# An arena of ten 16 KB pairs in place of twenty 8 KB blocks, with expert weights loaded four rows at a time

## The chip, the cores and the metric

One core of a Trainium2 chip. The time is device microseconds of one execution, the median of the runs; in the profile, times are microseconds from the start of the span unless marked ns.

## The reference, cut to what matters

One encoder layer for 256 tokens of width 1024, all in float32: two attention branches side by side, merged by gates, then 32 experts of which every token takes four.

```
mod = silu(c) @ w_ada + b_ada                      # 6 vectors: shift, scale, gate, twice
z = (x * (1 + scale1) + shift1) @ w_in             # q, k, v of A; compressed q, kv of B; two gates
y_a, y_b = chunked_attention(z), latent_attention(z)
merged = sigmoid(g_a) * (y_a @ w_branch_a) + sigmoid(g_b) * (y_b @ w_branch_b)
x = layer_norm(ALPHA * x + gate1 * (merged @ w_out))
h = x * (1 + scale2) + shift2
experts = top 4 of (h @ w_router + b_router), softmax weights
f = sum over the 4: weight * (swiglu(h @ w_gate[e], h @ w_up[e]) @ w_down[e])
out = layer_norm(ALPHA * x + gate2 * f)
```

The expert weights are 32 x 3 matrices of 1024 x 1024 float32, 4 MB each.

## The kernel before, in words

**The arena.** Nearly everything large that comes from memory, and many intermediates, live in one pool of `NB = 20` blocks of 8 KB per partition (1 MB each over 128 partitions). `al` takes the block that has been free longest (`freed` holds the count at which each was freed), `fr` gives blocks back, `hold(n)` sets n free blocks aside for a while. A load into a block waits for the last reader of what was in it before. Which block a load gets is settled when the program is written out; the order in which each engine's queue takes its instructions is set then too, by the framework's planner (`schedule_with_timeline_sim=True`), from its own estimate of times. All large loads are issued by SP, whose queue takes its instructions in order.

**Split matmuls.** In the mixers a float32 product is made of three matmuls of rounded halves (`mm3`, lines 278 to 281): `split` (lines 151 to 153) casts a block into a high part on ACT and subtracts it on DVE or POOL for the low part, so each weight block takes two more blocks.

**Mixers.** `load_start`, `modulate` and `project` make the first projections. Twelve `z_pair` steps follow, beside eight `attend` steps; each `ada2` step (line 627) loads two blocks of `w_ada`, which DVE adds into two accumulators `acc0` and `acc1` (line 640). The matmuls called `mod` (lines 706 and 707) reduce them, bank after bank, first the four of `acc0`, then those of `acc1`. Then `load_branch` (line 761) loads a quarter of both branch weights and splits it, four times, two ahead of the matmuls `ba` and `bb`; each quarter is merged with the gates `gT` (lines 796 to 799) into `mg`. `load_wo` (line 805) does the same with quarters of `w_out`; eight calls of `o_part` (line 836, two token halves, two column halves, two quarters) make `o`. Normalisation and routing follow, in a row of small steps.

**Experts.** All experts run as dense products over gathered tokens: group `s` of two experts, then `e0` to `e12` of two or three (`GROUPS`), each with the matrices `g`, `u` and `d` in turn. `load_group` (line 1006) issues the loads of one matrix of a group: for each of four quarters and each expert j one block of two rows per partition. A partition p holds the rows 8p to 8p+7 of a matrix, so two rows are 8 KB in one piece. `mm` (line 1056) goes through k = 0 to 7; each k takes 16 matmuls over the two column halves and the experts' token segments, and after every odd k it frees the blocks of that quarter:

```
                if k % 2 == 1:
                    for rg in regs:
                        fr(rg[k // 2])
```

After the `g` matrix of group `s`, `take_late` takes two blocks for good. The last load of the last group (`fine`) is cut in column halves. The loop over extra items (line 1322, `get_w`) runs only where an expert has more tokens than its slots.

Of the kernel before, what the change touches and what calls it, by code (L numbers as in the profile page):

```python
# [8 lines left out]
F32 = mybir.dt.float32  # L9
# [8 lines left out]
P = 128  # L18
# [14 lines left out]
NB = 20  # L33
# [37 lines left out]
def tile_layer(  # L71
# [49 lines left out]
    freed = {i: i - NB for i in range(NB)}  # L121
    clock = [0]

    def al(dt=F32):
        assert freed, "no block is free"
        i = min(freed, key=freed.get)
        del freed[i]
        clock[0] += 1
        return ar.tile([P, BLK], dt, tag=f"blk{i}", bufs=1, name=f"blk{i}_{clock[0]}"), i
# [9 lines left out]
    def fr(*blocks):  # L139
        for i in blocks:  # L140
            clock[0] += 1
            assert i not in freed
            freed[i] = clock[0]
# [60 lines left out]
    hTh_v, hTh_r = al(F32R)  # L204
    hTl_v, hTl_r = al(F32R)
# [109 lines left out]
    def project(b):  # L315
        wv = LS[b][1]
        ws = []
        for kk in range(2):
            hi, hr = al(F32R)
            lo, lr = al(F32R)  # L320
            split(wv[kk][0][:, 0:NZ], hi[:, 0:NZ], lo[:, 0:NZ], "VG"[kk])
            fr(wv[kk][1])
            ws.append((hi, lo, hr, lr))
        for kk in range(2):
            k = 2 * b + kk
            hi, lo, hr, lr = ws[kk]
# [4 lines left out]
            fr(hr, lr)  # L331
# [41 lines left out]
    def split_cols(L, n, pieces=2, engs="VG"):  # L373
        w, r = L
        hv, hr = al(F32R)
        lv, lr = al(F32R)
        hi = hv.rearrange("p (k m) -> p k m", k=8)
        lo = lv.rearrange("p (k m) -> p k m", k=8)
        st = 8 // pieces
        for i in range(pieces):  # L380
            sl = slice(i * st, (i + 1) * st)
            split(w[:, sl, :], hi[:, sl, :], lo[:, sl, :], engs[i % len(engs)])
        fr(r)
        return hi, lo, (hr, lr)
# [176 lines left out]
    yT, yT_r, gT, gT_r = [None, None], [], [], []  # L561

    def take_yT(br):
        v, r = al(F32R)
        yT[br] = v.rearrange("p (s j n) -> p s j n", s=2, j=4)
        yT_r.append(r)
# [77 lines left out]
    def z_pair(name, dst):  # L644
        W = split_cols(loads[name], 256, 4, "GVGG" if name[0] == "g" else "GVGV")
        ps = ps_g(name)
        for j in range(2):
            z_T(W, j, ps[:, j * S:(j + 1) * S])
        A.copy(dst, ps.rearrange("p (j n) -> p j n", j=2))
        fr(*W[2])  # L650
# [19 lines left out]
    fr(hTh_r, hTl_r, qk_r, bva[0][1], bva[1][1])  # L670
# [85 lines left out]
    hold(4)  # L756
# [4 lines left out]
    def load_branch(jp):  # L761
        v, r = al()
        v = v.rearrange("p (b k m) -> p b k m", b=2, k=4)
        for br, w in enumerate((w_branch_a, w_branch_b)):
            SP.dma_start(v[:, br, :, :], w[0].rearrange("(k p) m -> p k m", p=P)[:, :, jp * 256:(jp + 1) * 256])
        hv, hr = al(F32R)
        lv, lr = al(F32R)
# [5 lines left out]
        WB.append((hi, lo, hr, lr))  # L773
# [3 lines left out]
    mgh_v, mgh_r = al(F32R)  # L777
    mgl_v, mgl_r = al(F32R)
    mgh = mgh_v.rearrange("p (j n) -> p j n", j=8)
    mgl = mgl_v.rearrange("p (j n) -> p j n", j=8)  # L780
    for jp in range(4):
# [8 lines left out]
        fr(WB[jp][2], WB[jp][3])  # L790
# [9 lines left out]
    fr(*yT_r, *gT_r)  # L800
# [4 lines left out]
    def load_wo(hf, i):  # L805
# [3 lines left out]
        hv, hr = al(F32R)  # L809
        lv, lr = al(F32R)  # L810
# [6 lines left out]
        WO.append((hi, lo, hr, lr))  # L817
# [130 lines left out]
    for i in range(2):  # L948
        for t in range(2):
            o_part(t, 0, i)  # L950
        fr(*WO[i][2:4])
        load_wo(1, i)
# [7 lines left out]
    for i in range(2):  # L960
        o_part(1, 1, i)
        fr(*WO[2 + i][2:4])
# [18 lines left out]
    fr(mgh_r, mgl_r, rt_r, ms_r, rwa_r, rwb_r)  # L981
# [12 lines left out]
    def take_late():  # L994
        if not late:
            a, b = al()[0], al()[0]
# [30 lines left out]
    def expert_group(nm, segs, slots, wcol, get_w, get_bias, hooks=(), end=None):  # L1027
# [28 lines left out]
        def mm(stat, kind, name):  # L1056
# [4 lines left out]
            def step(k, hf):  # L1061
                for c0, m, par in segs:
                    T.matmul(pss[hf][c0:c0 + m, :], stat[:, k, c0:c0 + m],  # L1063
                             ch[par][k // 2][:, k % 2, hf * 512:(hf + 1) * 512],
                             start=(k == 0), stop=(fine and k == 7), skip_group_check=True)

            for k in range(8):
# [8 lines left out]
                if k % 2 == 1:  # L1076
                    for rg in regs:
                        fr(rg[k // 2])
# [230 lines left out]
    with tc.For_i(0, n_items) as it:  # L1309
# [60 lines left out]
```

## Time and profile before

| | |
|---|---|
| Runs | 1250.84, 1247.3, 1252.55 us; median 1250.84 |
| The profiled execution | 1245.99 us, span 1244.3 us |
| Mean granted TensorE clock | 0.966 of full speed |
| PE, DVE, ACT, POOL busy | 1103.0, 362.8, 172.5, 123.0 us |
| Bytes read from memory | 459.09 MB |
| Expert loads | 128 + 128 + 126 loads of 1,024 KB, 4 of 512 KB |

In a timeline a line gives start, duration, engine and line of the code, operation, the tile written and the tiles read, shape, and in square brackets the idle time before it with what ended it. All blocks of the arena appear as `blk`. A line of a group has busy time and mean duration in ns of one behind the first bar, and behind the second the idle time just before. `SPq` is the load queue. DMA share is the mean busy share of 16 DMA engines; it can exceed 1. The queue line of the packets gives packets, MB and that share.

### The profile page before, as it was taken

What the parts mean: (1) busy time and instruction counts of PE and PEld (TensorE: products, weight loads), DVE (VectorE), ACT (ScalarE), POOL (GpSimd) and SP (SyncE); (2) the same over time, 40 slices, a digit from 0 to 9 for tenths busy, and PEclk for the clock granted to TensorE, in tenths of its full rate; (3) what the DMA queues carried; (4) which work ended last, traced back from release to release, by engine and by line L of the source; (5) the groups of instructions that cost most, each with busy time, mean ns of one, the idle gap of its engine ahead of it and who ended that gap; (6) DMA issues with size and microseconds to landing.
All of it is one profiled execution on the core that took longest, in us unless ns stands there. A gap on an engine that the chain in (4) does not pass through costs nothing.

```text
span 1244.3 us, 19465 instructions
## 1 busy us (share of the span) xinstructions
PE 1103.0 (89%) x8023; PEld 511.9 (41%) x8023; DVE 362.8 (29%) x704; ACT 172.5 (14%) x340; POOL 123.0 (10%) x140
## 2 busy tenths in 40 slices
PE   6889999797998989899989789889889999899995
PEld 4658885773242433434223223232233434343431
DVE  4868982684121121211012001011011211111113
ACT  3345552230000000000000000000000000000011
POOL 2211562433000000000000000000000000000001
PEclk8989998898999999899999999999999999999998
DMA  9958646398999999999999999999999999999992
GB/s 341 345 186 307 229 142 237 102 355 333 421 420 420 421 422 420 422 420 420 421 421 421 421 420 421 422 421 420 422 421 421 421 420 421 420 420 421 421 399 76
DMA packets 90333, 461.44 MB, mean 371 GB/s; under 512 B 8809, under 2 KB 33430, under 8 KB 39298
## 3 DMA queue, kind: packets, MB, share of 16 engines
q1 hardware_dynamic: 90242, 460.17, 91.6%
q8 instruction: 64, 1.05, 0.3%
q14 instruction: 27, 0.22, 0.0%
HBM read 459.09 MB, written 1.05 MB: 370 GB/s over the span
## 4 chain that ended last, share of the span: by engine, by line
DMA 48%; PE 36%; DVE 8%; issue 3%; SPq 2%; ACT 1%; POOL 1%; DVEq 0%; ACTq 0%; POOLq 0%
DMA blk<-in_w_down_dram 19%; DMA blk<-in_w_up_dram 14%; DMA blk<-in_w_gate_dram 13%; DVE blk L640 1%; PE e2d L1063 1%; PE e0d L1063 1%; PE sg L1063 1%; PE e12d L1063 1%; PE e3d L1063 1%; PE e1d L1063 1%; PE sd L1063 1%; PE e3u L1063 1%; PE e2u L1063 1%; PE e1u L1063 1%; PE e0u L1063 1%
## 5 line engine op out<-in xcount | busy, mean ns | idle before, releaser
L153 POOL TENSOR_TENSOR blk<-blk,blk 128x512 fp32r<-128x512 f32 (+2 forms) x44 | 84.8, 1948 | 148.8 <-ACT blk L152 80.5
L1298 POOL COPY sel<-sel 96x64 bf16<-96x64 bf16 (+2 forms) x30 | 5.9, 230 | 807.5 <-PE e5d L1132 90.4
L152 ACT CAST blk<-blk 128x512 fp32r<-128x512 f32 (+2 forms) x76 | 54.1, 767 | 41.5 <-DVE blk L798 16.6
L1092 ACT ACTIVATE blk<-blk 128x512 f32<-128x512 f32 x28 | 17.2, 630 | 234.0 <-DVE blk L1090 234.0
L153 DVE TENSOR_TENSOR blk<-blk,blk 128x512 fp32r<-128x512 f32 (+2 forms) x32 | 39.0, 1227 | 33.7 <-ACT blk L152 23.0
L640 DVE SCALAR_TENSOR_TENSOR blk<-blk,csil,blk 128x1024 f32<-128x1024 f32 x28 | 41.8, 1537 | 1.3 <-DMA blk<-in_w_ada_dram 1.2
L281 PE MATMUL g<-blk,blk 128*128 128x256 f32 x128 | 36.6, 291 | 2.0 <-POOL blk L153 2.0
L279 PE MATMUL g<-blk,blk 128*128 128x256 f32 x128 | 36.8, 288 | 0.0
L280 PE MATMUL g<-blk,blk 128*128 128x256 f32 x128 | 36.1, 282 | 0.0
L1063 PE MATMUL e7u<-blk,xgb 128*32 128x512 f32 x128 | 25.3, 599 | 4.5 <-DMA blk<-in_w_up_dram 4.5
L1063 PE MATMUL e5u<-blk,xgb 128*32 128x512 f32 x128 | 25.6, 599 | 4.0 <-DMA blk<-in_w_up_dram 4.0
L1063 PE MATMUL e6u<-blk,blk 128*32 128x512 f32 x128 | 25.3, 599 | 4.0 <-DMA blk<-in_w_up_dram 4.0
L1063 PE MATMUL e5d<-blk,xgb 128*32 128x512 f32 x128 | 23.2, 656 | 3.6 <-DMA blk<-in_w_down_dram 3.4
L281 PEld LDWEIGHTS g<-blk,blk 128*128 128x128 f32 x128 | 24.2, 191 | 4.3 <-POOL blk L153 2.9
L1063 PE MATMUL e7d<-blk,blk 128*32 128x512 f32 x128 | 22.7, 597 | 3.0 <-DMA blk<-in_w_down_dram 2.7
L279 PEld LDWEIGHTS g<-blk,blk 128*128 128x128 f32 x128 | 24.5, 191 | 0.9 <-issue 0.6
L1063 PE MATMUL e6d<-blk,xgb 128*32 128x512 f32 x128 | 22.4, 621 | 2.5 <-DMA blk<-in_w_down_dram 2.5
L1063 PE MATMUL e4d<-blk,blk 128*32 128x512 f32 x128 | 22.1, 613 | 2.8 <-DMA blk<-in_w_down_dram 2.8
L280 PEld LDWEIGHTS g<-blk,blk 128*128 128x128 f32 x128 | 24.5, 191 | 0.0
L1063 PE MATMUL e4u<-blk,xgb 128*32 128x512 f32 x128 | 20.6, 596 | 2.0 <-DMA blk<-in_w_up_dram 2.0
L1063 PE MATMUL e6g<-blk,blk 128*32 128x512 f32 x128 | 19.4, 596 | 1.8 <-DMA blk<-in_w_gate_dram 1.8
L1063 PE MATMUL e7g<-blk,xgb 128*32 128x512 f32 x128 | 19.4, 595 | 1.7 <-DMA blk<-in_w_gate_dram 1.7
(745 smaller groups left out, 1919.2 us busy)
## 6 DMA issues: line engine op xcount, KB each, us to landing
blk<-in_w_gate_dram SPq DMA_DIRECT2D x128, 1024.0 KB, 19.7
blk<-in_w_up_dram SPq DMA_DIRECT2D x128, 1024.0 KB, 19.8
blk<-in_w_down_dram SPq DMA_DIRECT2D x126, 1024.0 KB, 19.8
blk<-in_w_ada_dram SPq DMA_DIRECT2D x24, 1024.0 KB, 9.6
blk<-in_w_in_dram SPq DMA_DIRECT2D x12, 1024.0 KB, 5.4
blk<-in_w_in_dram SPq DMA_DIRECT2D x8, 592.0 KB, 11.4
blk<-in_w_out_dram SPq DMA_DIRECT2D x4, 1024.0 KB, 6.0
blk<-in_w_branch_a_dram SPq DMA_DIRECT2D x4, 512.0 KB, 3.7
```

The source lines that it names most:

```text
L152: A.copy(hi, src)
L153: (V if eng == "V" else G).tensor_sub(lo, src, hi.bitcast(F32))
L279: T.matmul(o, sh, mh, start=first, stop=False)
L280: T.matmul(o, sh, ml, start=False, stop=False)
L281: T.matmul(o, sl, mh, start=False, stop=last)
L640: eng.scalar_tensor_tensor(acc_v[:, sl], v[:, q * D:(q + 1) * D], csil[:, k:k + 1], acc_v[:, sl], op0=ALU.mult, op1=ALU.add)
L1063: T.matmul(pss[hf][c0:c0 + m, :], stat[:, k, c0:c0 + m], ch[par][k // 2][:, k % 2, hf * 512:(hf + 1) * 512], start=(k == 0), stop=(fine an ...
L1092: A.activation(s, g[:, sl], AF.Sigmoid, scale=SW_ALPHA)
L1298: G.tensor_copy(sel[:, lo:lo + n], sel96[:, r:r + 1].to_broadcast([96, n]))
```

## The change

The arena becomes ten pairs of 16 KB per partition. `al2` takes a whole pair, the one free longest. `al` takes a half of a broken pair if there is one, the one freed first among these, else it breaks the next pair. `fr` joins two free halves to a pair again; `fr2` frees a pair. High and low part of a split come from one pair (`hi_lo`); both `yT` and the two late blocks are pairs too; `hold` counts pairs. Expert weights are loaded four rows per partition at a time, 16 KB in one piece and 2 MB a load, and freed after k = 3 and k = 7. In the last group's `fine` matrix the second half is loaded as two rows and then two column halves of two rows.

```diff
-    freed = {i: i - NB for i in range(NB)}
+
+    freed = {i: i - NB for i in range(0, NB, 2)}
+    half = {}
+    pair = {}
     clock = [0]

-    def al(dt=F32):
-        assert freed, "no block is free"
+    def al2(dt=F32):
+        assert freed, "no pair of blocks is free"
         i = min(freed, key=freed.get)
         del freed[i]
         clock[0] += 1
-        return ar.tile([P, BLK], dt, tag=f"blk{i}", bufs=1, name=f"blk{i}_{clock[0]}"), i
+        pair[i] = ar.tile([P, 2 * BLK], dt, tag=f"blk{i}", bufs=1, name=f"blk{i}_{clock[0]}")
+        return pair[i], i
+
+    def al():
+        if half:
+            i = min(half, key=half.get)
+            del half[i]
+        else:
+            i = al2()[1]
+            half[i + 1] = clock[0]
+        return pair[i & ~1][:, (i & 1) * BLK:(i & 1) * BLK + BLK], i
+
+    def fr2(*pairs):
+        for i in pairs:
+            clock[0] += 1
+            assert i not in freed and i % 2 == 0 and i not in half and i + 1 not in half
+            freed[i] = clock[0]
+
+    def fr(*blocks):
+        for i in blocks:
+            clock[0] += 1
+            assert i not in half and (i & ~1) not in freed
+            if i ^ 1 in half:
+                del half[i ^ 1]
+                freed[i & ~1] = clock[0]
+            else:
+                half[i] = clock[0]

...
-    def fr(*blocks):
-        for i in blocks:
-            clock[0] += 1
-            assert i not in freed
-            freed[i] = clock[0]
+    def hi_lo():
+        v, i = al2(F32R)
+        return v[:, 0:BLK], v[:, BLK:2 * BLK], i
...
-            hi, hr = al(F32R)
-            lo, lr = al(F32R)
+            hi, lo, hr = hi_lo()
...
-    yT, yT_r, gT, gT_r = [None, None], [], [], []
+    yT, gT, gT_r = [None, None], [], []
+    yT_v, yT_r = al2(F32R)
...
-    hold(4)
+    hold(2)
...
-        hv, hr = al(F32R)
-        lv, lr = al(F32R)
+        hv, lv, hr = hi_lo()
...
-        fr(WB[jp][2], WB[jp][3])
+        fr2(WB[jp][2])
...
-            a, b = al()[0], al()[0]
+            ab = al2()[0]
+            a, b = ab[:, 0:BLK], ab[:, BLK:2 * BLK]
...
-        for kq in range(4):
+        for kh in range(2):
             for j in range(n):
-                v, r = al()
-                v = v.rearrange("p (k n) -> p k n", k=2)
-                if not (fine and kq == 3):
-                    SP.dma_start(v, aps[j][:, 2 * kq:2 * kq + 2, :])
+                v, r = al2()
+                v = v.rearrange("p (k n) -> p k n", k=4)
+                if not (fine and kh == 1):
+                    SP.dma_start(v, aps[j][:, 4 * kh:4 * kh + 4, :])
+                else:
+                    SP.dma_start(v[:, 0:2, :], aps[j][:, 4:6, :])
                 ch[j].append(v)
                 regs[j].append(r)
         if fine:
             for hf in range(2):
                 sl = slice(hf * 512, (hf + 1) * 512)
                 for j in range(n):
-                    SP.dma_start(ch[j][3][:, :, sl], aps[j][:, 6:8, sl])
+                    SP.dma_start(ch[j][1][:, 2:4, sl], aps[j][:, 6:8, sl])
...
-                             ch[par][k // 2][:, k % 2, hf * 512:(hf + 1) * 512],
+                             ch[par][k // 4][:, k % 4, hf * 512:(hf + 1) * 512],
                              start=(k == 0), stop=(fine and k == 7), skip_group_check=True)

             for k in range(8):
@@ -1073,9 +1100,9 @@
                 elif not (fine and k == 7):
                     for hf in range(2):
                         step(k, hf)
-                if k % 2 == 1:
+                if k % 4 == 3:
                     for rg in regs:
-                        fr(rg[k // 2])
+                        fr2(rg[k // 4])
...
-            for kq in range(4):
-                v, r = al()
-                v = v.rearrange("p (k n) -> p k n", k=2)
-                SP.dma_start(v, src[:, 2 * kq:2 * kq + 2, :])
+            for kh in range(2):
+                v, r = al2()
+                v = v.rearrange("p (k n) -> p k n", k=4)
+                SP.dma_start(v, src[:, 4 * kh:4 * kh + 4, :])
```

## Rows read from the trace of the kernel before

**Rows 1.** The page: DMA rate in 40 slices; the chain that ended last.

```profile
GB/s 341 345 186 307 229 142 237 102 355 333 421 420 420 421 422 420 422 420 420 421 421 421 421 420 421 422 421 420 422 421 421 421 420 421 420 420 421 421 399 76
...
DMA 48%; PE 36%; DVE 8%; issue 3%; SPq 2%; ACT 1%; POOL 1%; DVEq 0%; ACTq 0%; POOLq 0%
```

**Rows 2.** By stage: PE, PEld, DVE, ACT, POOL busy; clock, DMA share, GB/s.

```profile
60.00:190.00 130.00, 121.81 (x870) 101.89 (x869) 109.84 (x212) 68.21 (x177) 51.72 (x34) 0.97 0.63 221
190.00:293.00 103.00, 83.27 (x440) 63.86 (x439) 62.33 (x124) 32.25 (x45) 45.34 (x28) 0.87 0.66 246
293.00:589.00 296.00, 276.81 (x2386) 108.28 (x2390) 56.56 (x122) 17.40 (x30) 2.77 (x14) 0.98 1.00 413
```

**Rows 3.** Waits of the load queue, 285 to 320 us.

```profile
SPq L1014 <- PE sg L1063: 7.3, 2, 7.0
```

**Rows 4.** DMA packets, 14 to 18 us, then 400 to 1200 us.

```profile
DMA packets 1387, 1.41 MB, mean 351 GB/s; under 512 B 18, under 2 KB 1386, under 8 KB 1387
...
q1 hardware_dynamic: 1387, 1.41, 110.2%
...
DMA packets 46166, 336.59 MB, mean 421 GB/s; under 512 B 5123, under 2 KB 5123, under 8 KB 5123
...
q1 hardware_dynamic: 46111, 335.79, 101.0%
```

**Rows 5.** Timeline of the load queue SP, 176 to 300 us.

```profile
189.20 0.40 SPq L765 DMA_DIRECT2D blk<-in_w_branch_a_dram  x1
...
220.15 0.37 SPq L765 DMA_DIRECT2D blk<-in_w_branch_a_dram  x1
...
236.56 14.31 SPq L808 DMA_DIRECT2D blk<-in_w_out_dram  x4
...
298.71 0.80 SPq L1014 DMA_DIRECT2D blk<-in_w_down_dram  x2
```

**Rows 6.** Timeline of PE: `sg` (293 to 312 us), last `e12u` matmuls.

```profile
293.40 8.72 PE L1063 MATMUL sg<-blk,xgb 128*32 128x512 f32 x63
...
1199.82 3.63 PE L1063 MATMUL e12u<-blk,blk 128*32 128x512 f32 x24 [0.58 <-DMA blk<-in_w_up_dram]
```

**Rows 7.** The chain in order of time: start, duration, what.

```profile
190.09 5.04 DMA blk<-in_w_branch_b_dram
...
352.59 13.78 PE e0g L1063 x128
```

**Rows 8.** Loads of `w_out` (L808), from issue to landing.

```profile
DMA to landing us min/median/max: 6.0/6.0/6.0
```

**Rows 9.** Groups by shape, 185 to 300 us: parts of `split`.

```profile
L153 POOL TENSOR_TENSOR blk<-blk,blk 128x1024 fp32r<-128x1024 f32 x8 | 21.8, 2723 | 30.7 <-ACT blk L152 19.7 <-issue 10.9
...
L152 ACT CAST blk<-blk 128x1024 fp32r<-128x1024 f32 x16 | 16.0, 1044 | 5.5 <-DMA blk<-in_w_out_dram 5.5
```

**Rows 10.** Timeline of POOL, 205 to 240 us.

```profile
207.35 2.37 POOL L153 TENSOR_TENSOR blk<-blk,blk 128x1024 fp32r<-128x1024 f32 x1 [10.87 <-issue]
...
229.84 8.62 POOL L153 TENSOR_TENSOR blk<-blk,blk 128x1024 fp32r<-128x1024 f32 x3 [7.74 <-ACT blk L152]
```

**Rows 11.** Timeline of PE: `mod`, the second branch pair, first and last `o`.

```profile
199.99 1.05 PE L706 MATMUL mod<-blk,ones 128*32 128x512 f32 x2
...
232.23 0.58 PE L281 MATMUL bb<-blk,blk 128*128 128x256 f32 x1 [8.92 <-POOL blk L153]
...
248.05 0.40 PE L279 MATMUL o<-blk,blk 128*128 128x512 f32 x1
...
269.89 0.39 PE L281 MATMUL o<-blk,blk 128*128 128x512 f32 x1
```

**Rows 12.** Timeline of ACT, 235 to 260 us: last merge's cast.

```profile
250.50 0.62 ACT L152 CAST blk<-blk 128x512 fp32r<-128x512 f32 x1 [0.18 <-DVE blk L798]
```

**Rows 13.** `ada2` loads (L630) to landing; their DVE steps, 60 to 191 us.

```profile
DMA to landing us min/median/max: 6.1/8.0/10.0
...
L640 DVE SCALAR_TENSOR_TENSOR blk<-blk,csil,blk 128x1024 f32<-128x1024 f32 x28 | 41.8, 1537 | 1.3 <-DMA blk<-in_w_ada_dram 1.2
```

More of the change, by code (lines that the diff above doesn't have):

```diff
@@ L203, in tile_layer @@
     xT = xT_v.rearrange("p (k n) -> p k n", k=8)
-    hTh_v, hTh_r = al(F32R)
-    hTl_v, hTl_r = al(F32R)
+    hTh_v, hTl_v, hT_r = hi_lo()
     hTh = hTh_v.rearrange("p (k n) -> p k n", k=8)
@@ L318, in project @@
         for kk in range(2):
-            hi, hr = al(F32R)
-            lo, lr = al(F32R)
+            hi, lo, hr = hi_lo()
             split(wv[kk][0][:, 0:NZ], hi[:, 0:NZ], lo[:, 0:NZ], "VG"[kk])
             fr(wv[kk][1])
-            ws.append((hi, lo, hr, lr))
+            ws.append((hi, lo, hr))
         for kk in range(2):
             k = 2 * b + kk
-            hi, lo, hr, lr = ws[kk]
+            hi, lo, hr = ws[kk]
             for pss, o, n in zsets:
@@ L330, in project @@
                     mm3(pss[t][:, 0:n], hTh[:, k, ts], hTl[:, k, ts], hi[:, o:o + n], lo[:, o:o + n], k == 0, k == 7)
-            fr(hr, lr)
+            fr2(hr)
     bias3 = [const.tile([96, D], BF, name=f"b3_{n}") for n in "gud"]
@@ L383, in split_cols @@
         fr(r)
-        return hi, lo, (hr, lr)
+        return hi, lo, hr
     def z_T(W, j, o):
@@ L560, in tile_layer @@
     kT = qk_v[:, 4 * S:8 * S].rearrange("p (j n) -> p j n", j=4)
-    yT, yT_r, gT, gT_r = [None, None], [], [], []
+    yT, gT, gT_r = [None, None], [], []
+    yT_v, yT_r = al2(F32R)
     def take_yT(br):
-        v, r = al(F32R)
+        v = yT_v[:, br * BLK:(br + 1) * BLK]
         yT[br] = v.rearrange("p (s j n) -> p s j n", s=2, j=4)
-        yT_r.append(r)
     def attend(br, hp):
@@ L649, in z_pair @@
         A.copy(dst, ps.rearrange("p (j n) -> p j n", j=2))
-        fr(*W[2])
+        fr2(W[2])
     take_yT(1)
@@ L669, in tile_layer @@
         ada2(4 + i)
-    fr(hTh_r, hTl_r, qk_r, bva[0][1], bva[1][1])
+    fr2(hT_r)
+    fr(qk_r, bva[0][1], bva[1][1])
     p2_cm.__exit__(None, None, None)
@@ L765, in load_branch @@
             SP.dma_start(v[:, br, :, :], w[0].rearrange("(k p) m -> p k m", p=P)[:, :, jp * 256:(jp + 1) * 256])
-        hv, hr = al(F32R)
-        lv, lr = al(F32R)
+        hv, lv, hr = hi_lo()
         hi = hv.rearrange("p (b k m) -> p b k m", b=2, k=4)
@@ L772, in load_branch @@
         fr(r)
-        WB.append((hi, lo, hr, lr))
+        WB.append((hi, lo, hr))
     load_branch(0)
     load_branch(1)
-    mgh_v, mgh_r = al(F32R)
-    mgl_v, mgl_r = al(F32R)
+    mgh_v, mgl_v, mg_r = hi_lo()
     mgh = mgh_v.rearrange("p (j n) -> p j n", j=8)
@@ L799, in tile_layer @@
         split(ga, mgh[:, js, :].rearrange("p a n -> p (a n)"), mgl[:, js, :].rearrange("p a n -> p (a n)"), "V")
-    fr(*yT_r, *gT_r)
+    fr2(yT_r)
+    fr(*gT_r)
     rt_v, rt_r = al()
@@ L808, in load_wo @@
         SP.dma_start(v, w_out[0, i * 512:(i + 1) * 512, hf * 512:(hf + 1) * 512].rearrange("(k p) m -> p k m", p=P))
-        hv, hr = al(F32R)
-        lv, lr = al(F32R)
+        hv, lv, hr = hi_lo()
         hi = hv.rearrange("p (k m) -> p k m", k=4)
@@ L816, in load_wo @@
         fr(r)
-        WO.append((hi, lo, hr, lr))
+        WO.append((hi, lo, hr))
     load_wo(0, 0)
@@ L950, in tile_layer @@
             o_part(t, 0, i)
-        fr(*WO[i][2:4])
+        fr2(WO[i][2])
         load_wo(1, i)
@@ L961, in tile_layer @@
         o_part(1, 1, i)
-        fr(*WO[2 + i][2:4])
+        fr2(WO[2 + i][2])
     r_T(0, 1)
@@ L980, in tile_layer @@
             weigh(t)
-    fr(mgh_r, mgl_r, rt_r, ms_r, rwa_r, rwb_r)
+    fr2(mg_r)
+    fr(rt_r, ms_r, rwa_r, rwb_r)
     p3_cm.__exit__(None, None, None)
```

## Prediction

> **What bounds the kernel now.** I read the page first. Its 40 slices show two kernels in one: up to slice 9 the DMA rate wanders between 102 and 355 GB/s, from slice 10 it stands at 420 to 422 until slice 38 [rows 1]. The chain that ended last says the same: DMA 48%, PE 36% [rows 1]. The table by stages fixes the borders [rows 2]: from 60 to 190 us PE is busy 122 of 130 us, with DVE at 110; from 190 to 293 neither PE (83 of 103) nor DMA (share 0.66) is full, so that stage is a chain of single steps; between 293 and 589 PE is busy 277 of 296 us and DMA moves 413 GB/s, so both are nearly full. Behind that the DMA alone sets the pace. The load queue's own waits come next: around 293 SP waits 7.0 us at once for PE's `sg` matmuls [rows 3]. That is the hand-over: all blocks are full when the experts begin, and no load leaves before PE frees one.
>
> So the end is the moment at which loads resume, plus the remaining weights at the DMA rate, plus a tail. What delays the first expert matmul delays the end one for one; what raises the rate pays over some 900 us.
>
> **Packets.** A load of two rows reads 8 KB in one piece per partition, four rows read 16 KB. Two stretches give the price of a packet [rows 4]. From 14 to 18 us, 1,368 packets (1,386 less 18 small) are of 1 KB: 4 us x 16 engines / 1,368 = 46.8 ns each. From 400 to 1200 us there are 46,111 - 5,123 = 40,988 of 8 KB: 312.3 ns each. A straight line through both gives 37.9 ns per KB and 8.9 ns per packet; 16 KB then costs 615.8 ns against 2 x 312.3, or 1.4% less. It applies to the loads after the hand-over except the last 6 MB, whose pieces stay as they are: 402.7 MB of experts (384 loads of 1,024 KB), less 18 MB there already, less 6 MB, about 377 MB, or 377 / 0.421 = 896 us (MB of a million bytes here, the blocks being 1.05 of them). **Gain 12.6 us.** Bounds: 0, if the rate depends on bytes alone, and 25.5 us, if the 8.9 ns vanish altogether. I take the straight line, since both its ends are measured.
>
> The rows thus show a cost per packet of 8.9 ns [rows 4]. The Trainium skill, "DMA: Bandwidth & Descriptors", section "Why small descriptors are slow", puts it at about 3 cycles per packet beside one cycle per 32 bytes, and counts joining descriptors as worth while only up to 256 bytes. By that, 8 KB takes 259 cycles, two of them 518 and 16 KB 515, a gain of 0.6% or 5 us, an estimate from that page; the sum below would come out 7 us higher. The rows show about twice the page's overhead, so the line through them stands.
>
> **Coarser frees.** PE now frees blocks after k=1, 3, 5 and 7 of a matrix, then only after k=3 and 7. At the hand-over `sg` starts at 293.40, its first 63 matmuls (k=0 to 3) take 8.72 us and end at 302.1, while today the first load left at 298.71 [rows 5, 6]. **+3.5 us** (bounds +2, if landings still run then, and +5). In the tail, PE today has 24 matmuls (3.63 us) left when the last `e12u` block lands [rows 6]; with two rows more per load it has some 62, at 0.108 us (13.78 / 128 [rows 7]) 6.7 us. Everything behind it up to the output follows in a row: **+3.1 us** (bounds 0 and 3.6). All other matrices have the next load in flight, which covers this.
>
> **Who waits for which block.** This is the part that costs. Today a freed block goes to the back of one list, so a new load gets the one longest idle. After the change `al` first takes a half of a broken pair, and the half freed last may be the only one. Followed through the program, the list gives:
> - The four branch loads (`load_branch`) all sit in one half block, the first after `acc0`, each next one after `split` has read the one before; so does `rt`. Today they use four blocks (after `ada2`, `hT`, `acc1`, `WB0`), and SP issues them between 189.20 and 220.15, all before use [rows 5].
> - `load_wo(0,0)` and `(0,1)` go into the halves of `gT0` and `gT1`, read until the last merge; `(1,0)` and `(1,1)` follow in the same halves after `split`. Today the first goes out at 236.56 [rows 5], while the branch matmuls still run.
>
> Prices: branch_b lands 5.04 us after its issue on the chain [rows 7], a `w_out` load after 6.0 [rows 8]; a cast of 128x1024 takes 1.04 us, the subtraction behind it on POOL 2.4 (2.37 the first of them, mean 2.72) [rows 9, 10].
>
> Loads 0 and 1 cost nothing. Load 0 must wait for the `mod` matmuls on `acc0` (to 200.0), is there at 205 and cast at 207.1; PE has three more banks of `mod` before it, and POOL begins its part at 207.35 today [rows 10, 11]. Load 1 leaves when POOL ends at 209.7 and is cast by 217, but POOL takes its low part only at 229.84, after the broadcasts of L745 [rows 10]. If that cover goes, the price is 5.04 each. Behind the waiting loads SP holds gate loads that are needed after 293, and loads of the same chain; nobody else waits. From there it is serial. Load 2 can leave at 232.2 (229.84 + 2.4): + 5.04 + 1.04 + 2.4 = 240.7. Load 3 leaves at 240.7: 245.7, cast 246.8, POOL 249.2, then 24 matmuls of 256 columns at 0.12 us (half of an `o` matmul's 22.1 / 96), so the branches end at 252.1, not 248.05, where `o` begins now [rows 11]: **+4.1 us**. The last merge ends 3.7 us after the branches, as today (248.05 to the cast at 250.50, 0.62 us, and a subtraction about as long) [rows 12], at 255.8. Only then `load_wo(0,0)` leaves: + 6.0 + 2 x 1.04 + 2.4 = 266.3 for its second half, five matmuls at 0.23 us more, and the first of eight `o` parts ends at 267.5. Seven more at 22.1 / 8 = 2.8 us (248.05 to 270.1 today [rows 11]) end at 286.9. The later two `w_out` loads need 266.3 + 6.0 + 2.1 + 2.4 = 276.8, just when PE reaches them (275.8). So `o` ends near 287 instead of 270.1, 16.9 us later, of which 4.1 are counted: **+12.8 us**. Bounds of the two together: 8 (other work is moved into the gaps, two casts overlap) and 26 (each chain also meets POOL's 8 to 11 us of idling).
>
> PE idles some 10 us in that gap. The granted clock of this stage is 0.87 on average [rows 2], so part of it already runs at 1.2 instead of 2.4 GHz; one more idle stretch brings one more such part: **+1 us** by estimate (0 to 5, if half of the 10 us follow at half speed).
>
> From 60 to 190 us the sixteen `ada2` loads and the gate loads also share few halves: one takes `k0`, two `ada2` loads, `g0`, three more, `g7`. A link is a landing of 8.0 us (10.0 at most) plus two DVE steps, 2.5 us together [rows 13]. From `k0` to `g0` that is 2 x 10.5 + 8 = 29 us, against three of the twelve projections in 130 us, 32.5; from `g0` to `g7` 3 x 10.5 + 8 = 39.5 against seven, 76. So they are hidden, the first just, and an `ada2` step that comes late holds up DVE, which takes its work in order (it waits 1.2 us for them today [rows 13]). **+2 us** (0 to 12). SP takes its loads in order, so a load behind a waiting one waits too; this is inside the upper bound. Indexing and `hold(2)` for `hold(4)` cost nothing: the same four blocks' worth is held, no instruction is added.
>
> **Sum:** -12.6 + 3.5 + 3.1 + 4.1 + 12.8 + 1 + 2 = +13.9 us. The profiled execution took 1245.99 us (span 1244.3 and 1.7 around it), so 1259.9; the median of the runs is 1250.84, 4.85 higher, so the forecast against it is 1264.7, a slowdown of 1.1%.
>
> **Rivals.**
> - *The half blocks are free of charge* (not slower). The place is the branch stage: PE stands there 8.92 us for POOL today [rows 11], so a later load may fall into waiting that exists. Then only -12.6 + 3.5 + 3.1 remain: 1244.8. It decides once all waits ahead of `sg` add up to less than about 6 us, and with another 0.3 us gained it passes the half per cent. Against it: `gT0` can't be overwritten before the merge. Chance 0.18.
> - *The packets get cheaper by half as much or not at all*, because part of the 8.9 ns belongs to the 1 KB packets alone (their DMA share is 1.10, that of the 8 KB ones 1.01 [rows 4]), or because the loads go out in the same pieces as before: 1264.7 + 6.3 to 12.6 = 1271 to 1277. For it: no load in the trace has 16 KB per partition. Against: nothing but their length tells the packets of the two stretches apart. Chance 0.12. By the Trainium skill's page named above it would be about the half.
> - *DMA starves while PE leads* (groups s to e3). Frees come 4 MB at a time; 24 MB freed by `sd`'s end last until about 362.6 (25.2 million bytes from 303.7 on, at 427 GB/s), the next free comes after half of `e0g`, at 352.4 + 7 [rows 7], and its data near 361: 1 to 2 us of margin. If that is gone, each of five groups loses about 2 us: 1275. Chance 0.08.
>
> The forecast's case has 0.62. Its own range, by the bounds, is 1253 to 1279; about 0.09 of it lies within half a per cent of before, which is what a measurement of this kernel can tell from no change (6.3 us). Of the first rival 0.10 is faster, 0.08 the same. Hence faster 0.10, same 0.17, slower 0.73; the range 1247 to 1284 leaves out half of the first rival and the far ends.
>
> **What would show it.** In the changed profile: packets under 8 KB as now and about 24,600 instead of 49,200 large ones; the rate from 400 to 1200 us at 427 GB/s; issues of `load_branch` near 232 and 241, of `load_wo` near 256; PE idle about 10 us before the first `o` matmul; `sg` starting near 313; DMA idle until `sg` has done k=3; 60-odd `e12u` matmuls after the last landing. `sg` starting before 300 would break the forecast, as would a rate of 421 or of 435.

## The result, and the profile after

After: 1269.57 us, median of 6 runs (1267.92 to 1271.2), against 1249.14 (6 runs) of the kernel before beside them: a ratio of 1.0164 (1.0142 to 1.0185), 20.4 us slower. The profiled execution took 1271.2 us (span 1269.5), before 1245.99 (1244.3); all rows below come from these two, whose spans are 25.2 us apart, 4.8 more than the medians. One run of e1 (1554.8 us) and five of the six of e3 were slow executions of their kernel: the ratio of e1 leaves its one out, and e3 is given none.

The page after (rate in 40 slices; chain that ended last; against [rows 1]):

```profile
GB/s 332 238 267 207 276 200 182 81 177 308 337 428 418 427 428 426 427 417 427 427 428 427 427 428 427 428 428 425 428 428 427 426 427 428 426 428 425 428 376 39
...
PE 51%; DMA 33%; DVE 9%; issue 3%; ACT 2%; POOL 1%; SPq 0%; DVEq 0%; POOLq 0%; ACTq 0%
```

The plateau is higher (427 for 421), but begins a slice later, and slices 2, 4 and 7 to 11 (the first being 1) are emptier. The stages after (columns as in [rows 2]), and the packets from 400 to 1200 us (as [rows 4]):

```profile
60.00:190.00 130.00, 121.97 (x868) 102.90 (x858) 106.25 (x206) 68.15 (x173) 48.08 (x32) 0.96 0.68 241
190.00:293.00 103.00, 78.40 (x399) 59.22 (x398) 38.42 (x64) 30.44 (x40) 32.60 (x22) 0.83 0.46 163
293.00:589.00 296.00, 269.45 (x2254) 112.92 (x2253) 75.69 (x180) 23.66 (x44) 17.37 (x19) 0.94 0.96 404
```

```profile
DMA packets 23448, 341.51 MB, mean 427 GB/s; under 512 B 2600, under 2 KB 2600, under 8 KB 2600
...
q1 hardware_dynamic: 23397, 340.75, 100.2%
```

From 190 to 293 us the DMA moved 163 GB/s where it had moved 246. Of the large packets, 23,397 - 2,600 = 20,797 took 800 us x 16 engines: 615.5 ns each, as the straight line of the prediction had it (615.8). The chain after, in order of time (start, duration, what; against [rows 6, 7]):

```profile
237.09 3.60 DMA blk<-in_w_branch_b_dram
...
244.27 3.36 DMA blk<-in_w_branch_b_dram
...
251.28 3.40 DMA blk<-in_w_branch_b_dram
...
264.08 6.63 DMA blk<-in_w_out_dram
...
322.03 8.96 PE sg L1090 x63
...
1220.48 7.06 PE e12u L1090 x56
```

Three branch loads and a `w_out` load now stand on the chain one after another, `sg` begins at 322.03 (293.40 before), and 56 matmuls are left behind the last `e12u` landing (24 before). The same events in both kernels:

| | before | after | later by |
|---|---|---|---|
| `cqT` begins (end of the first stage) | 66.7 | 79.0 | 12.3 |
| `mod` begins | 191.41 | 207.67 | 16.3 |
| `o` ends | 270.1 | 297.7 | 27.6 |
| `sg` begins | 293.40 | 322.03 | 28.6 |
| loads resume behind `sg` | 298.71 | 331.01 | 32.3 |
| last `e12u` landing | 1199.82 | 1220.48 | 20.7 |
| end of the span | 1244.3 | 1269.5 | 25.2 |

So 28.6 us are lost ahead of `sg`, 3.7 more at the hand-over, 11.6 come back through the faster packets, and 4.5 are lost in the tail. These are one execution of each, and the first stage varies: in six profiled kernels with the mixers of before, `cqT` (the first transposes behind the first projections) begins at 66.7 to 71.9 us, early where the granted clock from 40 to 60 us was 1.00 and late where it was 0.83 to 0.91; in seven with the mixers of the change it begins at 77.3 to 79.2. Of the 12.3 us of the first row, then, at least 5 are firm. From `cqT` to `mod` the kernels of either group agree within 0.8 us.

### The profile page after: what moved, and what is told of

Its sections match the earlier page's. It is cut to its first block, busy times and chain, and to the rows that moved or that the text cites. A ratio compares the mean times of both kernels' runs of the same rounds, so it can differ in the third digit from the quotient of the medians.

```text
span 1269.5 us, 18745 instructions
## 1 busy us (share of the span) xinstructions
PE 1082.6 (85%) x8023; PEld 515.2 (41%) x8023; DVE 359.1 (28%) x704; ACT 176.2 (14%) x342; POOL 121.9 (10%) x140
## 4 chain that ended last, share of the span: by engine, by line
PE 51%; DMA 33%; DVE 9%; issue 3%; ACT 2%; POOL 1%; SPq 0%; DVEq 0%; POOLq 0%; ACTq 0%
DMA blk<-in_w_up_dram 19%; DMA blk<-in_w_down_dram 11%; PE sg L1090 1%; PE e11d L1090 1%; PE e2d L1090 1%; PE e9d L1090 1%; PE e0d L1090 1%; PE e12d L1090 1%; PE e3d L1090 1%; PE e10d L1090 1%; PE sd L1090 1%; PE e8d L1090 1%; PE e3g L1090 1%; PE e8u L1090 1%; PE e1d L1090 1%
## 5 line engine op out<-in xcount | busy, mean ns | idle before, releaser
L180 POOL TENSOR_TENSOR blk<-blk,blk 128x512 fp32r<-128x512 f32 (+2 forms) x44 | 81.7, 1877 | 148.9 <-ACT blk L179 134.8
L307 PE MATMUL g<-blk,blk 128*128 128x256 f32 x128 | 37.9, 296 | 6.6 <-POOL blk L180 6.6
L305 PE MATMUL g<-blk,blk 128*128 128x256 f32 x128 | 37.7, 295 | 0.0
L306 PE MATMUL g<-blk,blk 128*128 128x256 f32 x128 | 37.5, 293 | 0.0
L307 PEld LDWEIGHTS g<-blk,blk 128*128 128x128 f32 x128 | 25.5, 199 | 7.2 <-POOL blk L180 7.0
L305 PEld LDWEIGHTS g<-blk,blk 128*128 128x128 f32 x128 | 25.5, 199 | 1.2 <-issue 1.1
L306 PEld LDWEIGHTS g<-blk,blk 128*128 128x128 f32 x128 | 25.4, 199 | 0.8 <-issue 0.8
L1090 PE MATMUL e5d<-blk,xgb 128*32 128x512 f32 x128 | 19.7, 654 | 6.3 <-DMA blk<-in_w_down_dram 6.0
L1090 PE MATMUL e6d<-blk,xgb 128*32 128x512 f32 x128 | 17.7, 594 | 5.8 <-DMA blk<-in_w_down_dram 5.5
L305 PE MATMUL o<-blk,blk 128*128 128x512 f32 x32 | 13.6, 435 | 10.6 <-ACT blk L179 10.6
```

The costliest lines, as they stand in the source:

```text
L180: (V if eng == "V" else G).tensor_sub(lo, src, hi.bitcast(F32))
L305: T.matmul(o, sh, mh, start=first, stop=False)
L306: T.matmul(o, sh, ml, start=False, stop=False)
L307: T.matmul(o, sl, mh, start=False, stop=last)
L1090: T.matmul(pss[hf][c0:c0 + m, :], stat[:, k, c0:c0 + m], ch[par][k // 4][:, k % 4, hf * 512:(hf + 1) * 512], start=(k == 0), stop=(fine an ...
```

## The experiments

One number sorts all of them: how many MB had landed by 400 us, from where on the DMA runs without a break in each. Before, 117.59 MB had, and by the last `e12u` landing 117.59 + 0.42074 x 799.8 = 454.1 MB. For every other kernel, 400 us plus (454.1 less its own MB by 400) over its own rate should be when its last `u` lands. (e6 and e12 load other pieces there; the last column is seen on the chain.)

| kernel | median us | ratio to before (95%) | span | MB by 400 | GB/s from 400 | `u` landed: worked out | seen |
|---|---|---|---|---|---|---|---|
| after | 1269.57 | 1.0164 (1.0142 to 1.0185) | 1269.5 | 104.08 | 427 | 1219.9 | 1220.5 |
| e1 mixers as before | 1256.18 | 1.0042 (1.0021 to 1.0064) | 1251.4 | 110.55 | 427 | 1204.2 | 1204.0 |
| e7 experts as before | 1283.4 | 1.0252 (1.0227 to 1.0277) | 1283.3 | 102.27 | 421 | 1236.3 | 1237.2 |
| e4 start in pairs | 1266.94 | 1.0128 (1.0101 to 1.0155) | 1262.2 | 107.18 | 427 | 1212.6 | 1212.1 |
| e5 staging in turns | 1271.26 | 1.0151 (1.0124 to 1.0179) | 1270.5 | 104.08 | 427 | 1219.5 | 1220.5 |
| e2 rows of two | 1281.2 | 1.0236 (1.0209 to 1.0262) | 1279.4 | 104.31 | 421 | 1231.3 | 1229.0 |
| e9 split rows | 1280.52 | 1.0235 (1.0207 to 1.0264) | 1278.7 | 104.56 | 421 | 1230.6 | 1230.5 |
| e8 rows of one | 1308.22 | 1.0452 (1.0422 to 1.0482) | 1306.6 | 103.67 | 408 | 1259.6 | 1255.8 |
| e10 placed | 1252.17 | 1.0009 (0.9985 to 1.0033) | 1249.0 | 112.71 | 427 | 1199.2 | 1199.1 |
| e11 sort behind `sg` | 1244.59 | 0.9947 (0.9925 to 0.9969) | 1240.2 | 116.15 | 427 | 1191.5 | 1192.0 |

The sum holds within about 1 us, except for e2 and e8, which land 2 and 4 us sooner. So two things set when the last `u` lands: what had landed by 400 us, and the rate. Behind it the tail takes another 44 to 51 us.

### What makes the rate: pieces, not loads

**e2: two loads of two rows.**

```diff
-                    SP.dma_start(v, aps[j][:, 4 * kh:4 * kh + 4, :])
+                    for q in range(2):
+                        SP.dma_start(v[:, 2 * q:2 * q + 2, :], aps[j][:, 4 * kh + 2 * q:4 * kh + 2 * q + 2, :])
```

> Edit: the kernel after, with each 2 MB expert load made as two loads of 1 MB, of two rows of each partition (8 KB pieces in place of 16 KB); blocks and frees as after. Theory (the rate comes from the size of a piece): packets of 8 KB at 312.3 ns, 421 GB/s in place of 427, so 1269.6 + 12 = 1281 us (1278 to 1285). Rival (the rate comes from fewer and larger loads, or the change of rate is not what the last landing shows): the same as the next kernel's. Should loads of half the size let TensorE begin earlier on each piece, 3 us come off at the tail.

Measured: 1281.2 us.

**e9: one load of 2 MB in 8 KB pieces** (`ROWS = (0, 1, 4, 5, 2, 3, 6, 7)`).

```diff
+                src = aps[j].rearrange("p (a b k) n -> p b a k n", a=2, b=2)
-                    SP.dma_start(v, aps[j][:, 4 * kh:4 * kh + 4, :])
+                    SP.dma_start(w, src[:, kh])
...
-                    T.matmul(pss[hf][c0:c0 + m, :], stat[:, k, c0:c0 + m],
+                    T.matmul(pss[hf][c0:c0 + m, :], stat[:, ROWS[k], c0:c0 + m],
```

> Edit: the kernel after, with the two pairs of an expert's matrix loaded as rows 0, 1, 4, 5 and rows 2, 3, 6, 7 of each partition: as many loads as after, 2 MB each, but every partition's part comes in two pieces of 8 KB; the matmuls take the rows in that order. Theory (a time per piece): packets near 312 ns, 421 GB/s, 1281 us (1278 to 1285), as the kernel with 1 MB loads of two rows. Rival (the size or the number of loads sets the rate): 615 ns for 16 KB, or 308 for 8 KB, 427 GB/s, 1267 to 1272.

Measured: 1280.52 us. Packets of e9, then of e2, from 400 to 1200 us:

```profile
DMA packets 43620, 336.66 MB, mean 421 GB/s; under 512 B 2566, under 2 KB 2566, under 8 KB 2566
...
q1 hardware_dynamic: 43570, 335.92, 101.0%
```

```profile
DMA packets 46171, 336.62 MB, mean 421 GB/s; under 512 B 5123, under 2 KB 5123, under 8 KB 5123
...
q1 hardware_dynamic: 46118, 335.85, 101.0%
```

e9 has half the small packets of e2, since it has half as many loads; the large ones are 41,004 and 40,995, 312.2 ns each in both. As many loads as after, and yet the rate of before: the piece decides, the load doesn't.

**e8: four loads of one row** (as e2, with 4 and 1).

> Edit: the kernel after, with each 2 MB expert load made as four loads of one row of each partition (4 KB pieces). Theory (a fixed time per piece): 615.5 ns for 16 KB and 312.3 for 8 KB give 9.1 ns a piece beside 303.2 for 8 KB, so 160.7 ns for 4 KB, 408 GB/s, and over some 404 MB of expert weights about 404000/408 - 404000/427 = 44 us more than 1269.6: 1305 to 1316 us. Rival (the gain at 16 KB has another cause than a time per piece, as a pairing of pieces): 1281 to 1290, like 8 KB.

Measured: 1308.22 us. Its queue from 400 to 1200 us:

```profile
DMA packets 89398, 326.12 MB, mean 408 GB/s; under 512 B 9929, under 2 KB 9929, under 8 KB 89338
...
q1 hardware_dynamic: 89338, 325.30, 102.3%
```

79,409 packets of 4 KB, 161.2 ns each, where the line through the other two gave 160.7. From 4 to 8 KB, 151.0 ns are added, so 10.2 of the 161.2 go with the packet and not with its bytes; from 8 to 16 KB it is 9.1.

**e3: two loads of half the partitions each, pieces of 16 KB.**

```diff
-                    SP.dma_start(v, aps[j][:, 4 * kh:4 * kh + 4, :])
+                    for q in range(2):
+                        SP.dma_start(v[64 * q:64 * q + 64], aps[j][64 * q:64 * q + 64, 4 * kh:4 * kh + 4, :])
```

> Edit: the kernel after, with each 2 MB expert load made as two loads of 1 MB, each of 64 partitions with four rows (16 KB pieces kept); as many loads as in the kernel before. Theory (the rate comes from the size of a piece, not from the size or number of loads): 615 ns a packet, 427 GB/s, and 1269.6 us (1266 to 1273). Rival (the number of loads sets the rate): 1281, as the kernel with two rows. Rival (64 partitions use the engines unevenly): above 1290.

Measured: 1955.94 us (1843 to 2150, 6 runs). It tells nothing on the number of loads, because something larger came in; e9 was made for that question. The packets of the profiled execution, which took 2094.34 us, from 400 to 1200 us:

```profile
DMA packets 13549, 177.54 MB, mean 222 GB/s; under 512 B 2710, under 2 KB 2710, under 8 KB 2710
...
q1 hardware_dynamic: 13520, 177.12, 100.8%
```

10,810 packets of 16 KB, 1,184 ns each: nearly twice 615.5, with all 16 engines still shown busy.

### Where the loss is made: mixers and experts apart

**e1: mixers as before, experts as after.**

```diff
-        fin_v, o_v = al()[0], al()[0]
+        fo = al2()[0]
...
+    ar_cm.__exit__(None, None, None)
+    ar2 = ctx.enter_context(tc.tile_pool(name="ar2", bufs=1, side="left", reuse_waits="tile"))
+    freed2 = {i: max(freed[i], freed[i + 1]) for i in range(0, NB, 2)}
```

(against before; `al2` and `fr2` serve the experts from `ar2`, with the loads of the change.)

> Edit: the mixers keep the 20 blocks of 8 KB of the kernel before; that arena ends behind the last staged matrix of the mixers, and a second arena of 10 pairs of 16 KB serves the experts with the 2 MB loads of the change. Theory (the loss of the change is made ahead of `sg`, by whole pairs and shared pairs in the mixers, and the experts alone gain by the larger packets): the kernel before 1249.1, less 11.7 (last e12u landing, after against before, with the later start taken off), plus 3.7 (loads resume later behind coarser frees), plus 4.6 (longer tail) = 1245.7 us, between 1241 and 1252 since the pairs of the second arena are ready when both of their blocks are; `sg` near 293 and large packets near 615 ns. Rival A (the loss lies in the coarser expert pieces): 1262 or more with `sg` near 293. Rival B (the packets gain nothing once the mixers are as before): 1249.1 + 3.7 + 4.6 = 1257.

Measured: 1256.18 us. 13 of the 20 us are gone and rival A falls; but that is 10.5 us above the theory's sum. It is also close to rival B's 1257, but rival B falls by the rate: from 400 us on e1 runs at 427 GB/s, as after the change, so the packets do gain. The load queue's waits of e1 from 190 to 330 us, the stretch from 285 to 295 us, and the chain:

```profile
SPq L1036 <- POOL x_sb L935: 12.0, 1, 12.0
```

```profile
285.00:295.00 10.00, 5.10 (x24) 4.51 (x23) 8.40 (x8) 1.61 (x6) 10.00 (x5) 0.50 0.01 2
```

```profile
298.85 0.98 PE tokT L1190 x4
...
302.82 16.32 PE sg L1087 x128
```

For 10 us the DMA moves nothing (2 GB/s): SP waits for a pair. `rt`, `ms`, `rwa` and `rwb` live until the routing ends, in four blocks of four different pairs, so they hold 8 MB where before they held 4. And the planner has put the sort (`tokT`, which puts the experts in order) ahead of `sg`; before, it stands behind the first 64 of its matmuls:

```profile
302.20 0.39 PE L1166 MATMUL tokT<-ident,posm 128*32 128x128 f32 x2
```

**e7: mixers as after, experts as before** (second arena of 20 blocks behind the mixers).

> Edit: the other half, mixers on 10 pairs as in the change, experts on 20 blocks with the 1 MB loads of the kernel before. Theory (loss ahead of `sg`): `sg` begins near 322 as after the change, and the rest takes as long as before: 1249.1 + 28.6 = 1277.7 us (1272 to 1283), large packets near 312 ns each. Rival (the loss is made in the experts' coarser pieces): 1249 to 1255. If e1 and this one add up (e1 minus before, plus this minus before, equals 20), the two halves of the change act one after the other.

Measured: 1283.4 us, 5.7 above the sum and just above its range. Its chain shows where they are:

```profile
323.59 0.98 PE tokT L1211 x4
...
327.55 16.62 PE sg L1108 x128
```

Here too the sort stands ahead of `sg`, which begins at 327.5, 5.5 us later than after the change. The rival falls. The halves don't add up (5.0 + 32.2 against 20.4). Both arrangements with a second arena have the sort ahead of `sg`; what that costs was tried in e11, on e1's side alone.

**e10: the last blocks of the mixers placed by a list** (against e1):

```diff
-        i = min(freed, key=freed.get)
+        i = next(plan) if planned else min(freed, key=freed.get)
...
-    hold(4)
+    hold(18, 19, 10, 11)
```

> Edit: e1, with the last blocks of the mixers placed by a list, so that blocks that come free together are neighbours: the two blocks of a pair of the second arena then end at the same time (the four that live until the routing ends share two pairs in place of four). Theory (the end is set by how much the DMA has loaded by the time it runs without a break; e1 stood at 110.5 MB by 400 us where before stood at 117.5, since pairs with one live half kept the arena full and the DMA idle from 285 to 295 us): 113 to 117 MB by 400 us, the idle stretch gone or halved, and the time below e1's 1256.2 by (MB gained) / 0.427, that is 1241 to 1251 us, likeliest 1247. Rival (`sg` starts late for its place in TensorE's order, behind `tokT`, and that sets it): `sg` still near 302.8 and 1253 to 1257.

Measured: 1252.17 us, 112.71 MB by 400 us: both just outside what the theory gave, on the rival's side, though `sg` begins at 298.3 and not at 302.8. The stretches of e10 from 285 to 315 us (last columns: clock, DMA share, GB/s), and its chain:

```profile
285.00:295.00 10.00, 2.68 (x37) 1.99 (x35) 8.56 (x25) 1.61 (x6) 5.64 (x3) 0.69 0.79 313
295.00:305.00 10.00, 9.23 (x56) 3.91 (x58) 1.97 (x7) 0.00 (x0) 1.37 (x4) 0.63 0.69 294
305.00:315.00 10.00, 10.00 (x94) 3.20 (x90) 0.38 (x1) 0.00 (x0) 0.00 (x0) 1.00 0.25 81
```

```profile
294.38 0.98 PE tokT L1192 x4
```

The hole at 285 is filled, and a new one opens at 305 to 315 (81 GB/s). First all pairs are full until `sg` frees one with its 64th matmul, near 307.4. But the next load leaves only at 311.73, and in the meantime the load queue itself is at work: it reads the numbers of the 30 sorted experts, one after the other, which the later loads need as addresses (SP's loads, then line 1312 of e10):

```profile
311.73 0.34 SPq L1038 DMA_DIRECT2D pr<-in_w_down_dram  x1
...
L1312 SPq TENSOR_LOAD <-order_i x30: 262/266/468, 294.6 to 312.6; - x30
```

All but one of these reads lie ahead of that load, about 17 us in a row. So the sort's place costs twice: it delays `sg`, and it lets SP begin its reads before the loads that wait for `sg`. In e1 the reads run from 299.1 to 316.6, and the next load leaves at 316.72.

The medians of e1 and e10 are 4 us apart (1.0042 and 1.0009, the intervals overlap). The profiled execution of e10 began late (`cqT` at 71.6, in e1 at 67.6); counted from there, `sg` begins 8.4 us sooner than in e1. What is left hangs on the sort's place, as the rival had it.

**e11: the sort bound behind `sg`** (against e10):

```diff
-                    hooks[(name, k)]()
+                    with tc.issue_after(last_mm[0].ins):
+                        hooks[(name, k)]()
```

> Edit: the placed kernel, with the sort's matmuls (`tokT`, `tokp`) bound to come behind the first 64 matmuls of `sg` on TensorE, as they stand before. Theory: `sg` begins 5.5 us earlier (near 297 where e1 had 302.7), frees its first pair as much earlier, and the time falls by 2 to 5 us against the placed kernel. Rival (the DMA has other pairs to fill then): no difference.

Measured: 1244.59 us, 0.9947 (0.9925 to 0.9969) of before. The same stretches, and the chain:

```profile
295.00:305.00 10.00, 10.00 (x94) 3.19 (x90) 1.81 (x8) 0.00 (x0) 0.00 (x0) 0.95 0.99 394
305.00:315.00 10.00, 10.00 (x92) 3.85 (x88) 3.68 (x10) 1.26 (x2) 0.87 (x4) 1.00 0.99 405
```

```profile
293.49 3.06 PE sg L1091 x13
...
301.94 0.54 PE tokT L1195 x4
```

`sg` begins 5 us sooner, the hole is closed (405 GB/s), 3.4 MB more have landed by 400 us, and its time is below both kernels'. The medians of e10 and e11 are 7.6 us apart, more than the 2 to 5 expected: SP's reads now begin at 302.7, behind the first two loads (301.84 and 302.26). How much of it is the earlier `sg` and how much the reads was not tried apart. This is the change's loading with the blocks of the mixers left as before, but for the last few.

### The start and the staging, in the kernel after

**e4: `xT` and the biases share the first pair.**

```diff
-    xT_v, xT_r = al()
+    xb_v, xT_r = al2()
+    xT_v = xb_v[:, 0:BLK]
...
-        v, r = al()
+        v, r = xb_v[:, BLK:2 * BLK], xT_r + 1
```

> Edit: in the kernel after, `xT` and the raw biases share the first pair, so that the two halves of w_ada, and the two row blocks of w_in, of each step of the start share one pair and come free together. Theory (the 12.2 us that are lost by 79 us come from pairs shared by w_ada and w_in halves with other lives): the last `gemvT` near 53 to 56 instead of 63.4, cqT done near 67 to 70 instead of 79.0, and the time 1269.6 - 8 to 12 = about 1259 us (1256 to 1263). Rival (the next stage waits for its own half blocks, and swallows it): cqT early, `mod` still near 207, time 1267 to 1271. Rival (the start is late for another reason, as the order of the biases on VectorE): cqT near 79 and 1269.

Measured: 1266.94 us, above the 1256 to 1263 of the theory. The interval of its ratio overlaps with the one after; the medians are 2.6 us apart, the profiled spans 7.3 (e4's is its fastest run, the one after its slowest). `cqT` begins at 68.5, 10.5 us sooner and far from the 77.3 to 79.2 of the kernels with the start of the change, so the start is as expected: sharing pairs between `w_ada` and `w_in` halves makes it late. But `mod` begins at 203.7, only 4.0 sooner than after. Of PE's waits from 66 to 208 us in e4 the longest is

```profile
PE g L308 <- POOL blk L180: 11.6, 1, 11.6
```

where after shows 6.1 at most on that line. So the next stage takes back 6.5 of the 10.5 us, much as the first rival said.

**e5: branch and `w_out` loads take turns on a pair of their own.**

```diff
-    hold(2)
+    hold(1)
+    st_v, st_r = al2()
...
-        v, r = al()
-        v = v.rearrange("p (b k m) -> p b k m", b=2, k=4)
+        v = turn_st().rearrange("p (b k m) -> p b k m", b=2, k=4)
```

> Edit: in the kernel after, the loads of the branch weights and of w_out take turns on the two halves of one pair of their own (one of the two held pairs), instead of the one free half block that each of them waits for. Theory (the branch and W_out staging is a chain load, split, load, split over one half block): the time from `mod` to the end of `o` falls from 90.0 to about 80 us (before: 78.7), and the kernel from 1269.6 to about 1260 us (1257 to 1264); the wait of TensorE ahead of the first `o` falls from 10.6 to under 3 us. Rival (the pairs for hi and lo hold it back too, or the one held pair less delays the first expert loads by as much): 1265 to 1270.

Measured: 1271.26 us, no gain. The loads do come sooner (the last branch load leaves at 241.03, after the change at 251.28), but `mod` to the end of `o` takes 94 us. Waits of e5 from 200 to 325 us:

```profile
DVE b1s L774 <- POOL blk L770: 26.9, 1, 26.9
...
PE gb L753 <- DVE wrsum L752: 22.8, 1, 22.8
```

With other blocks the planner wrote another order: on POOL the broadcasts of L770 stand late, DVE waits for them, and PE's small `gb` matmul, which waits for DVE, now blocks the branch matmuls behind it. So this run doesn't show what the half-block chain alone costs.

### The tail

**e6 and e12: the second half of `u` in two loads**, of the last group (on e1) and of the last three (on e11).

```diff
-                if not (fine and kh == 1):
+                if not ((fine or late_u) and kh == 1):
...
+        if late_u:
+            for j in range(n):
+                SP.dma_start(ch[j][1][:, 2:4, :], aps[j][:, 6:8, :])
```

> Edit: e1 (mixers as before, experts in pairs), and the second half of the last group's `u` weights is loaded as rows 4 and 5, then rows 6 and 7. Theory (the tail is 56 matmuls behind the last `u` landing in place of 24): the 56 fall to about 24, from 7.06 to 3.6 us, and the time is that of e1 less 3.4 us. Rival (the `d` weights land next and set the end): e1 less 0 to 1 us, with TensorE waiting in `e12d` instead.

> Edit: the kernel with the sort behind `sg`, and the second half of the `u` weights of the last three groups loaded as rows 4 and 5, then rows 6 and 7. Theory (behind a coarse `u` landing TensorE has 56 matmuls left, 7.06 us, in place of 24 of 3.63 us, and runs without a wait from the `u` of the last group but one to the end, as in e6): 2 to 4 us less than the same kernel without it. Rival (only the last group counts, or the `d` loads end as late): 0 to 1 us.

Measured: e6 1257.67 us, 1.0047 (1.003 to 1.0065), against e1's 1.0042; e12 1242.28, 0.9942 (0.9918 to 0.9966), against e11's 0.9947. No difference can be told in either pair. The chain of e6:

```profile
1200.05 13.89 PE e12u L1090 x128
```

All 128 matmuls run in one piece: TensorE no longer waits for the last `u`, since it is itself behind; its last wait for a load was in `e11u`, whose 56 matmuls were left as they were. In e12 that one is split too, and a wait for a `d` load in `e11d` is the last (waits of PE from 1040 us on):

```profile
PE e11d L1094 <- DMA pr<-in_w_down_dram: 2.4, 1, 2.4
```

What the split brings is below what these runs can tell.

## Why the prediction was right, and by which terms

Sign and size were right (1264.7 forecast, 1269.57 measured, inside the range), but the closeness is partly luck: one stage was left out, which cost 12.3 us between the profiled executions, and another was put 6.6 us too high. Between the profiled spans:

| term | forecast | measured | from |
|---|---|---|---|
| larger packets | -12.6 | -11.6 | landing +20.7, loads resume +32.3 |
| coarser frees at the hand-over | +3.5 | +3.7 | 32.3 - 28.6 |
| tail | +3.1 | +4.5 | 25.2 - 20.7 |
| first stage | none | +12.3 | `cqT` |
| attention, 60 to 190 us | +2 | +4.0 | 16.3 - 12.3 |
| branch and `w_out`, with clock | +17.9 | +11.3 | 27.6 - 16.3 |
| routing | none | +1.0 | 28.6 - 27.6 |
| sum | +13.9 | +25.2 | |

**Packets, hand-over.** Right in mechanism and size, and shown: e2, e9 and e8 lie on the line of 8.9 ns and 37.9 ns per KB. The rival that packets get cheaper by half falls. From 8 to 16 KB the longer piece still brought 1.5% (307.8 ns per 8 KB in place of 312.3). The Trainium skill, "DMA: Bandwidth & Descriptors", section "Why small descriptors are slow", has a fixed overhead of about 3 cycles per packet, and calls joining descriptors into packets worth while only up to 256 bytes. That the overhead is fixed agrees with the runs; the limit is not one for the length of a piece, as the 1.5% show.

**The first stage is the step that failed.** The prediction followed half blocks from the attention on, and gave the stretch up to 60 us no term. There four steps each load two halves of `w_ada`; PE multiplies them (`gemv`), DVE copies the result (`md`), and PE turns it (`gemvT`). Timeline of DVE after:

```profile
34.39 0.68 DVE L371 CAST blk<-blk 96x1024 bf16<-96x1024 f32 x1
...
49.02 0.68 DVE L376 CAST b_d<-blk 32x1024 bf16<-32x1024 f32 x1
49.73 0.69 DVE L329 COPY md<-gemv 128x512 f32<-128x512 f32 x1
...
60.77 0.69 DVE L329 COPY md<-gemv 128x512 f32<-128x512 f32 x1 [6.54 <-PE gemv L325]
```

After the change `al` takes a freed half ahead of a free pair, so the second half of the third `w_ada` step goes into a block of the first step and waits for it; before, it went into a block not used yet. It was issued at 24.86 us (16.51 before). The second half of the third `gemv` begins at 41.87 (34.50 before), and the planner has put the bias work (34 to 49.7 us) ahead of the third `md` copy, at 49.73 (35.64 before). PE waits for that copy:

```profile
PE gemvT L332 <- DVE md L329: 8.5, 2, 7.5
```

The fourth follows at 60.77 (51.75 before). e4 undoes the sharing of pairs at this place alone and brings `cqT` back to 68.5. So the sharing is shown to be the cause. It works less by a late load (PE waits 0.2 us for `w_ada` up to 82 us) than by the order that the planner wrote for these loads; in e4 the third copy stands ahead of the bias work again, as before (DVE before, then in e4):

```profile
35.64 0.69 DVE L303 COPY md<-gemv 128x512 f32<-128x512 f32 x1 [0.21 <-PE gemv L299]
...
36.86 0.69 DVE L330 COPY md<-gemv 128x512 f32<-128x512 f32 x1 [0.60 <-PE gemv L326]
```

The same walk along the free list, begun at the first allocation, would have found the shared pairs, though not the planner's answer to them.

**Attention** was undersized, within its bounds (0 to 12). From `cqT` to `mod` it took 124.5 to 125.2 us in the six kernels with the mixers of before and 128.2 to 128.7 in the seven with those of the change, so the 4 us are firm. In e4 it took 135.2; why it gives back most of the earlier start, and which of its half blocks cost the 4 us, was not tried.

**Branch and `w_out`.** The chain is there as described: load, cast, POOL, load. Waits of PE, then of the load queue, after:

```profile
PE o L305 <- ACT blk L179: 10.6, 1, 10.6
```

```profile
SPq L790 <- POOL blk L180: 24.4, 3, 17.3
...
SPq L832 <- DVE blk L821: 11.0, 1, 11.0
```

The first row is the "some 10 us" of the forecast; the 11.0 is the first `w_out` load, which waits for the last merge as forecast. The part cost 11.3 and not 17.9: from `mod` to the first `w_out` load it took 55.0 us (191.41 to 255.8 in the forecast, 64.4), and from there to the end of `o` 35.0 (31.1). The forecast had tied load 2 to the date of POOL's broadcasts in the kernel before, 229.84; `mod` came 16 us late, but loads 2 and 3 of `branch_a` left at 237.56 and 245.35 and the first of `w_out` at 262.70, only 5 to 7 us after their dates (232, 241, 256). Those of `branch_b`, forecast with them, left 6 to 7 us behind each (244.27 and 251.28). That this chain alone costs 11 us wasn't shown, since e5 broke it and got another order.

**Tail.** 7.06 - 3.63 = 3.4 us are the 56 matmuls (62 forecast); the rest goes with the clock: `e12hT` took 1.95 us (1.13 before) and the first six `e12c` 3.40 (2.58), at a granted clock of 0.76 from 1229 to 1236 us, where before had 1.00 from 1206 to 1211.

**Half blocks free of charge** (the rival at 1244.8) was wrong for the change, but its sum is close to what e11 measures with the mixers left alone: 1244.59 us. Its single terms weren't taken apart there. **DMA starving** between groups falls: no slice from 12 to 38 is below 417 GB/s.

## What to carry to other kernels

Where transfers set the end, count the bytes landed by the moment at which they run without a break: that count and the rate gave the last landing of eight kernels within 1 us. Coarser buffers pay in the rate and cost in who shares a buffer with whom, so pair what comes free together, from the first allocation on. Where a planner writes the queues, a change of buffers also changes the order on every engine: compare the orders before blaming the waits, that of the load queue too, where small reads can stand ahead of a load.

## What the runs showed of the hardware

Loads of 64 partitions, alternating between the halves, ran at 222 GB/s in the profiled execution of e3 (2094.34 us), 0.52 of the 427 of 128 partitions, with the same 16 KB pieces. Its fastest run (1843.21 us) must have had more: with 86 MB landed by 400 us and a tail of some 46 us as in the other kernels, 264 GB/s, an estimate from these rows. The Trainium skill, "SBUF — State Buffer", section "Door 1: The DMA port swizzle", says that the rate depends on how many of the memory's 16 DMA ports the partitions reach, and 64 neighbours reach half of them. The trace agrees nearly, 1,184 ns a packet against 615.5. No run here shows why two loads in flight, one for each half, don't make up for it.
